# Fourier part of a DiT layer: first group's products copied to SBUF by ScalarE too, differences at another place, reversals and halves moved within the hand-written order

## The chip, the cores and the metric

The kernel runs on one core of one Trainium2 chip. The metric is the device time of one execution in microseconds (us), taken as the median of three runs; the time before is 2893.03 us (2890.24 to 2895.41). A profiled execution gives the rows that are read here: busy times, waits, DMA issues and landings, and the clock that the throttle grants to TensorE.

## What is computed

One layer of a hybrid diffusion backbone, for two streams: 256 prompt tokens and 2048 latent tokens of width 1024. The normalised and modulated input is projected to queries, keys, values and 512 Fourier channels. Four heads of differential attention work on the first three, four groups of 128 channels of a Fourier mixing on the last; both are joined by an output projection, and a squared-ReLU MLP follows. All inputs and outputs are float32. The part that the change touches computes this:

```python
def fourier_mix(f, w_four):
    b, n, _, _ = f.shape
    spec = jnp.fft.fft2(f.astype(jnp.float32), axes=(1, 3), norm='ortho').real.astype(f.dtype)
    return jnp.einsum('bngc,gce->bnge', spec, w_four).reshape(b, n, FOUR_WIDTH)
```

`n` is 256 for the prompt and 2048 for the latent tokens, which are transformed separately.

## The kernel before

The program goes through its stages in order: projection of 18 token tiles of 128 rows (to about 478 us), the Fourier part (to about 537 us), attention (its first product is L1020), then output projection and MLP. Most products of large size are made of three fp32r terms (L88 to L90); the Fourier part uses fp32 matmuls, which run in two passes, so that one 128x512 product shows as two MATMUL rows.

**Folding.** The transform over 2048 positions is a product with cosine and sine matrices. Sums and differences of mirrored and of distant rows split it into smaller ones, named by their size: "2048" (odd part, with the row halves E and DR made at the end of the projection), "e" (1024), "f" (512) and "l" (256). The prompt's 256 rows are the part "p". For the folding, DVE makes the differences `d1024` of the loaded sums `ss` (function diff, L792), the sums (summed, L795), and from a reversal of the rows on PE (reverse, L806 and L808, with the exchange matrices jm and k0) the halves e and o (even_odd, L816, L817, and a copy of one row, L819).

**A part's steps.** For each channel group g of a part, PE makes two position products (pabo at L733 for the 2048-row part, pabe and pabf at L745, pabp and pabl at L753), ScalarE copies them to SBUF (L737, L755), and one step later in the order yT makes two products over channels, py (L698) and pz (L700), whose difference and sum are the rows of the result and of its mirror image. ScalarE copies py to yu (L704). For group 0 of the 2048-row part DVE reads pz from PSUM: yd = yu - pz (L717) and yu = yu + pz (L718); POOL and DVE then write the four quarters of ys0 (L720 to L723). For groups 1 to 3 ScalarE copies pz to yv as well (L707), and the work on yu and yv is put on a list, LATE, and run at a later point of the order; for group 3 it is done by POOL. In the smaller parts DVE reads pz from PSUM at once (L712, L713). The results of the prompt, yp0 to yp3, are stored by POOL's DMA queue as each is ready (L763), those of the latent tokens at the end (L774).

**PSUM.** py, pz, the reversals and the two transposed tiles pt of the last token tile's queries and keys (head_T2, L847) share three buffers of the tag "y". A new tile has to wait until the last reader of the tile that had its buffer is done. The products pabo, pabe and so on have five buffers of their own.

**What sets the order.** From `with tc.manual_schedule()` on, instructions are issued as they are written, so each engine runs its instructions in that order. A table, AFTER, says what is done behind which step: ("o", g) is behind group g of the 2048-row part, ("p", g) behind group g of the prompt part, ("p", 0, 0) ahead of the last results of the part before. SBUF tiles take places that tiles of the projection had; a tile's first write waits for the last reader of what lay there, also where that reader is a store to DRAM. Stores of the last token tiles (queries qd at L355, keys kd at L341, values vd at L370 and vs at L378) stand in SP's queue, and so do the loads of attention (K at L966, V at L972, Q at L994).

Of the kernel before, what the change touches and what calls it, by code (L numbers as in the profile page):

```python
# [11 lines left out]
F32 = mybir.dt.float32  # L12
# [7 lines left out]
P = 128  # L20
D = 1024
KD = D // P
NP = 256
# [18 lines left out]
def body(tc, a, out):  # L42
    nc = tc.nc
    ctx = ExitStack()
    with ctx:
# [184 lines left out]
        with ExitStack() as c1:  # L230
# [358 lines left out]
            with tc.manual_schedule():  # L589
# [12 lines left out]
                def ft32(pool, tag, nm, bufs):  # L602
                    return pool.tile([P, 512], F32, tag=tag, name=nm, bufs=bufs)
# [82 lines left out]
        with ExitStack() as c2:  # L686
            ft = c2.enter_context(tc.tile_pool(name="f_t", bufs=2, reuse_waits="tile"))
            yp = c2.enter_context(tc.tile_pool(name="f_y", bufs=1, reuse_waits="tile"))
            fw = c2.enter_context(tc.tile_pool(name="f_w", bufs=1, side="right", reuse_waits="tile"))
            pp = c2.enter_context(tc.tile_pool(name="f_p", bufs=2, space=PSUM, reuse_waits="tile"))  # L690
            ys = [yp.tile([P, NS], F32, tag=f"ys{g}", name=f"ys{g}") for g in range(4)]
# [2 lines left out]
            def yT(dst, g, A, B, w, mirror_dst, parity=False):  # L694

                r = cw[g]
                py = pp.tile([P, 512], F32, tag="y", name="py", bufs=3)
                nc.tensor.matmul(py[:, :w], r[:, 0, :], A[:, :w], start=True, stop=True)  # L698
                pz = pp.tile([P, 512], F32, tag="y", name="pz", bufs=3)
                nc.tensor.matmul(pz[:, :w], r[:, 1, :], B[:, :w], start=True, stop=True)  # L700

                late = w == 512 and g > 0
                u, v = (fw if late else ft).tile([P, 512], F32, tag="yl" if late else "yu", name="yu", bufs=3 if late else 2)[:, :w], pz[:, :w]
                nc.scalar.copy(u, py[:, :w])  # L704
                if late:
                    v = fw.tile([P, 512], F32, tag="yv", name="yv", bufs=3)
                    nc.scalar.copy(v, pz)  # L707

                def go():
                    if not parity:  # L710
                        c = slice(1, P) if w == HW else slice(0, w)
                        nc.vector.tensor_sub(dst, u, v)  # L712
                        nc.vector.tensor_add(mirror_dst, u[:, c], v[:, c])  # L713
                        return
                    d = ft.tile([P, 512], F32, tag="yd", name="yd", bufs=2)
                    V = nc.gpsimd if g == 3 else nc.vector
                    V.tensor_sub(d, u, v)  # L717
                    V.tensor_add(u, u, v)  # L718
                    de, do, se, so_ = d[:, 0:256], d[:, 256:512], u[:, 0:256], u[:, 256:512]
                    nc.gpsimd.tensor_add(dst[:, 0:256], de, do)  # L720
                    nc.gpsimd.tensor_sub(mirror_dst[:, 511:255:-1], de, do)
                    V.tensor_sub(dst[:, 511:255:-1], se, so_)
                    V.tensor_add(mirror_dst[:, 0:256], se, so_)  # L723

                LATE.append(go) if late else go()
# [32 lines left out]
            HW = P + 1  # L758

            def put_prompt(g, A, B):  # L760
                y = ft.tile([P, NP], F32, tag="yp", name=f"yp{g}", bufs=4)
                yT(y[:, 0:HW], g, A, B, HW, y[:, NP - 1:P:-1])
                nc.gpsimd.dma_start(four[g * P:g * P + P, 0:NP], y)  # L763

# [65 lines left out]
            def late():  # L830
                LATE.pop(0)()

            AFTER = {("o", 0): [(diff, 1024, t) for t in (3, 2, 0, 1)],
                     ("o", 1): [(s_prompt,), (load_mats, "c1024", "s1024", "c512", "s512")],
                     ("o", 3): [(late,), (reverse, 512, 0), (even_odd, 512, 0)],
                     ("p", 0, 0): [(reverse, 512, 1), (even_odd, 512, 1)],
                     ("p", 1): [(summed, 1024, 1), (summed, 1024, 3)], ("p", 2): [(fold, 512, 1)],
                     ("p", 3): [(summed, 1024, 0), (summed, 1024, 2), (fold, 512, 0)],
                     ("e", 0): [(reverse, 256, 0), (late,)], ("e", 1): [(even_odd, 256, 0), (late,)], ("e", 3): [(s_last,)]}

            def after(*at_):
                for fn, *args in AFTER.get(at_, ()):
# [7 lines left out]
            with tc.manual_schedule():  # L850

                ptq = [pp.tile([P, 512], F32, tag="y", name=f"pt{LAST}_{m}", bufs=3) for m in range(2)]
                d1024 = [ft32(ft, "d", f"d1024_{t}", 4) for t in range(4)]
                mats = {nm: [fw.tile([P, a[nm].shape[1]], F32, tag=f"{nm}_{t}", name=f"{nm}_{t}", bufs=1)
                             for t in range(a[nm].shape[0] // P)] for nm in ("c512", "s512", "c1024", "s1024", "c256", "s256")}

                jm, k0 = (fw.tile([P, P], F32, tag=x, name=x) for x in ("jm", "k0"))
                for t in (jm, k0):
                    nc.gpsimd.memset(t, 0.0)
                nc.gpsimd.tensor_copy(jm[:, 1:P], ident[:, P - 1:0:-1])  # L860
                nc.gpsimd.tensor_copy(k0[:, 0:1], ident[:, 0:1])
                pws, paE = [pab("w0")], [pab(f"E{g}") for g in range(4)]
                pws.append(pab("w1"))

                def group_mats(h):
                    for j in range(2):
                        nc.tensor.matmul(pws[h][:, j * 256:j * 256 + P], c128, wf[:, 2 * h + j, :], start=True, stop=True)
                        nc.tensor.matmul(pws[h][:, j * 256 + P:j * 256 + 256], s128, wf[:, 2 * h + j, :], start=True, stop=True)

                def group_parts(h):  # L870
                    r = fw.tile([P, 2, 2, P], F32, tag=f"cw{h}", name=f"cw{h}")
                    nc.scalar.copy(r, pws[h].rearrange("p (g t c) -> p g t c", g=2, t=2))
                    cw.extend(r[:, j] for j in range(2))

                A = [None] * 4

                def e_evac(g):
                    A[g] = evac(paE[g], 0, 512, f"E{g}")

                for t in EROWS:  # L880
                    for g in range(4):
                        ab2048(paE[g], g, t, E[t], com[t], t == EROWS[0], t == EROWS[-1])
                    if t == 2:
                        group_mats(0)
                        group_parts(0)
                group_mats(1)
                e_evac(0)
                group_parts(1)
                e_evac(1)
                load_mats("c256", "s256")  # L890
                pend = None
                for g in range(4):
                    pa = pab(f"o{g}_1")
                    for t in ROWS:
                        ab2048(pa, g, t, DR[t][1], som[t], t == 0, t == 3)
                    B = evac(pa, 1, 512, f"o{g}_1")
                    if g < 2:
                        e_evac(g + 2)
                    if pend:
                        put(2048)(*pend)  # L900
                    pend = g, A[g], B
                    if g in (0, 2):
                        parts[1 - g // 2] = head_T2(g // 2, ptq[g // 2])
                    after("o", g)
                last_put = put(2048)
                for n, (ea, ma, eb, mb), w, p in (
                        ("p", (None, "c256", None, "s256"), HW, put_prompt),
                        ("e", (lambda: EO[512, "e"], "c1024", lambda: EO[512, "o"], "s1024"), 256, put(1024)),
                        ("f", (lambda: EO[256, "e"], "c512", lambda: EO[256, "o"], "s512"), 128, put(512)),
                        ("l", (None, "c256", None, "s256"), HW, put(256))):  # L910
                    for g in range(4):
                        if n in "pl":
                            nA, nB = (ab_half(g, q, (PR, S3)[n == "l"], MT[m][0], n) for q, m in enumerate((ma, mb)))
                        else:
                            nA = ab(g, 0, ea(), MT[ma], w, n)
                            nB = ab(g, 1, eb(), MT[mb], w, n)
                        after(n, g, 0)
                        last_put(*pend)
                        last_put, pend = p, (g, nA, nB)
                        if n == "p" and g == 0:  # L920
                            k_store(0, NK[0] // P - 1, parts[0])
                        if n == "e" and g == 0:
                            q_store(LAST, parts[1])
                        after(n, g)
                last_put(*pend)
# [7 lines left out]
        with ExitStack() as c3_:  # L933
# [265 lines left out]
            u = T / 5.0  # L1199
# [868 lines left out]
```

## Time and profile before

| what | value |
|---|---|
| runs of before | 2890.24, 2893.03, 2895.41 us, median 2893.03 |
| the profiled execution's own time | 2891.59 us |
| its span, first to last instruction | 2889.5 us |
| mean granted TensorE clock | 0.998 |
| busy share of the span | PE 99%, weight loads 85%, DVE 70%, ACT 53%, POOL 37% |
| DMA | 492.93 MB, 170 GB/s over the span |
| first product of attention | 537.08 us |

The span is 2.1 us shorter than the profiled execution's own time, and that time lies 1.4 us under the median of the runs. In the rows, PE is TensorE's matmul stream, DVE is VectorE, ACT is ScalarE, POOL is GpSimd and SP the engine that issues most DMAs; "SPq" and "POOLq" are their DMA issues. A row gives its start, its duration, the engine, the line, the output and the inputs by tile name, and in square brackets how long the engine had been idle and what ended that.

### The profile page before, as it was taken

How to read it: one execution, taken by the hardware profiler on the slowest of the kernel's cores; microseconds unless marked ns; L12 is line 12 of the kernel's file. 1: busy time of each engine (PE TensorE's matmuls, PEld its weight loads, DVE VectorE, ACT ScalarE, POOL GpSimd, SP SyncE). 2: the span in 40 equal slices, each digit the busy share in tenths (PEclk: the TensorE clock that was granted, in tenths of full speed). 3: DMA queues.
4: the chain of work that ended last, by engine and by line, in shares of the span. 5: the costliest groups of instructions: out<-in, count | busy, mean ns of one | idle time of the engine just before them, and what ended most of it. 6: DMA issues, size and time to landing. Idle time of an engine off the chain costs nothing.

```text
span 2889.5 us, 43210 instructions
## 1 busy us (share of the span) xinstructions
PE 2848.0 (99%) x15119; PEld 2468.9 (85%) x15119; DVE 2010.1 (70%) x3375; ACT 1545.7 (53%) x3502; POOL 1060.6 (37%) x869
## 2 busy tenths in 40 slices
PE   8999999999999999999999999999999999999999
PEld 4888787688888888888889999999998888888887
DVE  6676776898998989964478777778775354345554
ACT  4333322699898989953356566556554332233221
POOL 1112113599999999942223333333332000000000
PEclk9999999999999999999999999999999999999999
DMA  7777887521221212136777676667757464445563
GB/s 283 199 200 194 228 212 215 205 103 32 75 80 45 107 43 85 34 112 205 227 227 227 223 250 223 215 225 234 234 170 253 146 200 134 136 142 183 199 208 109
DMA packets 392779, 492.93 MB, mean 171 GB/s; under 512 B 26467, under 2 KB 306384, under 8 KB 389490
## 3 DMA queue, kind: packets, MB, share of 16 engines
q1 hardware_dynamic: 387136, 479.73, 52.6%
q0 software_dynamic: 1872, 7.28, 0.7%
q10 hardware_dynamic: 3554, 3.17, 0.4%
q8 instruction: 119, 1.95, 0.3%
q14 instruction: 98, 0.80, 0.1%
HBM read 312.58 MB, written 179.59 MB: 170 GB/s over the span
## 4 chain that ended last, share of the span: by engine, by line
PE 89%; DVE 4%; DMA 3%; ACT 2%; issue 1%; POOL 1%; SPq 1%; ACTq 0%; DVEq 0%; POOLq 0%
PE Ss L1020 10%; PE ps L89 8%; PE ps L88 8%; PE ps L90 8%; PE pts L1075 5%; PE po L90 4%; PE po L88 4%; PE po L89 4%; PE pj L88 3%; PE pj L89 3%; PE pj L90 3%; PE pA L1683 2%; PE pA L1684 2%; PE pB L1683 2%; PE pB L1684 2%; PE pB L1685 2%
## 5 line engine op out<-in xcount | busy, mean ns | idle before, releaser
L1025 DVE TENSOR_REDUCE mxs<-Ss 128x1 f32<-128x512 f32 x636 | 413.2, 685 | 63.1 <-PE Ss L1020 51.1
L1360 DVE TENSOR_TENSOR sl<-sr,sh 128x768 fp32r<-128x768 f32 x168 | 161.7, 964 | 337.8 <-ACT sh L1359 337.3
L1060 POOL TENSOR_TENSOR P0s<-P0s,P1s 128x1024 f32<-128x1024 f32 (+2 forms) x128 | 378.5, 2957 | 10.7
L1359 ACT CAST sh<-sr 128x768 fp32r<-128x768 f32 x168 | 140.2, 836 | 424.8 <-PE ps L89 423.9
L1725 POOL TENSOR_TENSOR gs<-g,g 128x384 f32<-128x384 f32 x48 | 69.7, 1451 | 469.7 <-ACT g L1695 419.0
L1044 ACT ACTIVATE P1s<-Ss,mxs 128x512 f32<-128x512 f32 x318 | 215.2, 694 | 36.2 <-DVE mxs L1028 36.2
L88 PE MATMUL pj<-wh,hh 128*128 128x512 f32 x576 | 229.4, 398 | 3.9 <-DVE qn L289 3.2
L89 PE MATMUL ps<-tlT,sh 128*128 128x512 f32 x585 | 229.4, 392 | 0.0
L88 PE MATMUL ps<-thT,sh 128*128 128x512 f32 x585 | 229.1, 392 | 0.0
L89 PE MATMUL pj<-wl,hh 128*128 128x512 f32 x576 | 227.7, 395 | 0.6 <-DVE wl L524 0.6
L90 PE MATMUL ps<-thT,sl 128*128 128x512 f32 x585 | 227.8, 389 | 0.0
L90 PE MATMUL pj<-wh,hl 128*128 128x512 f32 x576 | 226.9, 395 | 0.0
L1044 ACT ACTIVATE P0s<-Ss,mxs 128x512 f32<-128x512 f32 x318 | 214.1, 690 | 5.5 <-DVE mxs L1028 4.8
L1020 PE MATMUL Ss<-KS1s,Qs 128*128 128x512 f32 x636 | 196.2, 420 | 6.0 <-ACT P0s L1044 3.4
L1020 PE MATMUL Ss<-KS0s,Qs 128*128 128x512 f32 x636 | 195.5, 420 | 2.6 <-ACT P1s L1044 2.4
L1075 PEld LDWEIGHTS pts<-ident,P0s 128*128 128x128 f32 x1280 | 157.7, 140 | 42.6 <-ACT ahs L1082 2.2
L1075 PE MATMUL pts<-ident,P0s 128*128 128x128 f32 x1280 | 190.4, 272 | 0.7 <-ACT P1s L1044 0.7
L1694 ACT ACTIVATE g<-uz 128x384 f32<-128x384 f32 x144 | 75.8, 527 | 201.1 <-DVE uz L1717 171.4
L1059 POOL TENSOR_SCALAR P1s<-P1s,tots 128x1024 f32<-128x1024 f32 (+2 forms) x128 | 171.7, 1341 | 5.8
L1087 DVE TENSOR_TENSOR als<-pts,ahs 128x512 fp32r<-128x512 f32 x256 | 165.9, 681 | 6.9 <-ACT ahs L1082 6.6
L88 PE MATMUL ps<-ophT,sh 128*128 128x512 f32 x423 | 165.8, 392 | 1.1 <-DVE uz L1717 1.1
L90 PE MATMUL ps<-ophT,sl 128*128 128x512 f32 x423 | 165.8, 392 | 0.0
(533 smaller groups left out, 8057.1 us busy)
## 6 DMA issues: line engine op xcount, KB each, us to landing
sr<-sd SPq DMA_DIRECT2D x84, 768.0 KB
a<-in_w SPq DMA_DIRECT2D x184, 256.0 KB
sd<-gs SPq DMA_DIRECT2D x192, 192.0 KB
sd<-g SPq DMA_DIRECT2D x144, 192.0 KB
wm<-in_w_mod SPq DMA_DIRECT2D x32, 512.0 KB
Qs<-qd SPq DMA_DIRECT2D x32, 512.0 KB
b<-in_w SPq DMA_DIRECT2D x64, 256.0 KB
b<-tsum SPq DMA_DIRECT2D x64, 256.0 KB
```

The source lines that it names most:

```text
L88: nc.tensor.matmul(ps, lh, rh, start=first, stop=False)
L89: nc.tensor.matmul(ps, lh, rl, start=False, stop=False)
L90: nc.tensor.matmul(ps, ll, rh, start=False, stop=last)
L1020: nc.tensor.matmul(S[:, :w], self.Q[:, x, m, j * P:j * P + P], self.hd.KS[m][:, b * 512:b * 512 + w], start=(x == 0), stop=(x == 1))
L1025: nc.vector.tensor_reduce(self.mx[j][:, m, b:b + 1], self.S[j, m, b], axis=AX.X, op=ALU.max)
L1044: nc.scalar.activation(dst, S, AF.Exp, bias=self.mx[j][:, m, 6:7], accum_out=self.sm[j][:, m, b:b + 1])
L1059: nc.gpsimd.tensor_scalar(p, p, tot[:, 3:4], 0.0, op0=ALU.mult, op1=ALU.add)
L1060: nc.gpsimd.tensor_add(d, d, p)
L1075: nc.tensor.transpose(pt[:, c:c + P], self.p0[j][:, (kb + t) * P:(kb + t + 1) * P], ident)
L1087: nc.vector.tensor_sub(t, self.pt[kb], f32(self.A[kb][0]))
L1359: nc.scalar.copy(hi, src)
L1360: nc.vector.tensor_sub(lo, src, f32(hi))
```

## The change

Six edits, all in the Fourier part:

- The tiles yu and yv of the 2048-row part come from a new pool f_l with four buffers each, and `late` holds for group 0 as well: ScalarE copies its pz to yv, and its sums and differences go onto the list LATE, which is run at ("o", 1), behind the prompt's halves.
- The four result tiles of the prompt, YP, are allocated ahead of the differences d1024, in the same pool. By the addresses of the built programs the differences of before lie where vo17 lay, the value tile of the last token tile, which SP stores to vs at L378. Now YP lies there, and the differences lie where qn17 lay. The first Q tile of attention overlaps the place that YP has now.
- In AFTER, the reversal and the halves of 512 part 0 go from ("o", 3) to ("o", 2), those of part 1 from ("p", 0, 0) to ("o", 3), ahead of the LATE entry there; the sums and folds go up by about one step of the prompt part; the 256 reversal goes from ("e", 0) to ("p", 3), its halves from ("e", 1) to ("e", 0).

Behind L688 the lines of the changed kernel are one higher, behind L853 two.

```diff
             yp = c2.enter_context(tc.tile_pool(name="f_y", bufs=1, reuse_waits="tile"))
+            yl = c2.enter_context(tc.tile_pool(name="f_l", bufs=4, reuse_waits="tile"))
...
-                late = w == 512 and g > 0
-                u, v = (fw if late else ft).tile([P, 512], F32, tag="yl" if late else "yu", name="yu", bufs=3 if late else 2)[:, :w], pz[:, :w]
+                late = w == 512
+                u, v = (yl if late else ft).tile([P, 512], F32, tag="yu", name="yu", bufs=4 if late else 2)[:, :w], pz[:, :w]
                 nc.scalar.copy(u, py[:, :w])
                 if late:
-                    v = fw.tile([P, 512], F32, tag="yv", name="yv", bufs=3)
+                    v = yl.tile([P, 512], F32, tag="yv", name="yv", bufs=4)
                     nc.scalar.copy(v, pz)
...
             def put_prompt(g, A, B):
-                y = ft.tile([P, NP], F32, tag="yp", name=f"yp{g}", bufs=4)
+                y = YP[g]
...
-                     ("o", 1): [(s_prompt,), (load_mats, "c1024", "s1024", "c512", "s512")],
-                     ("o", 3): [(late,), (reverse, 512, 0), (even_odd, 512, 0)],
-                     ("p", 0, 0): [(reverse, 512, 1), (even_odd, 512, 1)],
-                     ("p", 1): [(summed, 1024, 1), (summed, 1024, 3)], ("p", 2): [(fold, 512, 1)],
-                     ("p", 3): [(summed, 1024, 0), (summed, 1024, 2), (fold, 512, 0)],
-                     ("e", 0): [(reverse, 256, 0), (late,)], ("e", 1): [(even_odd, 256, 0), (late,)], ("e", 3): [(s_last,)]}
+                     ("o", 1): [(s_prompt,), (late,), (load_mats, "c1024", "s1024", "c512", "s512")],
+                     ("o", 2): [(reverse, 512, 0), (even_odd, 512, 0)],
+                     ("o", 3): [(reverse, 512, 1), (even_odd, 512, 1), (late,)],
+                     ("p", 0): [(summed, 1024, 1), (summed, 1024, 3)], ("p", 1): [(fold, 512, 1)],
+                     ("p", 2): [(summed, 1024, 0), (summed, 1024, 2)], ("p", 3): [(fold, 512, 0), (reverse, 256, 0)],
+                     ("e", 0): [(even_odd, 256, 0), (late,)], ("e", 1): [(late,)], ("e", 3): [(s_last,)]}
...
                 ptq = [pp.tile([P, 512], F32, tag="y", name=f"pt{LAST}_{m}", bufs=3) for m in range(2)]
+                YP = [ft.tile([P, NP], F32, tag="yp", name=f"yp{g}", bufs=4) for g in range(4)]
                 d1024 = [ft32(ft, "d", f"d1024_{t}", 4) for t in range(4)]
```

On PE only three reversals move. This is PE's order before, from the products over channels of group 1 (py, pz) to the second reversal; pt17_1 is a transposition of the last token tile, pabo3 the position products of group 3, rev512 the reversals and fps, fpd the prompt's halves:

```order
L700 MATMUL pz_4784<-abo1_1_4748,cw0_4700 128x512
L847 MATMUL pt17_1_4663<-ident_175,qo17_1_4504 128x128 x4
L733 MATMUL pabo3_1_4798<-s20480_4505,rv0_4514 128x256
...
L698 MATMUL py_4805<-abE2_4729,cw1_4716 128x512
L700 MATMUL pz_4807<-abo2_1_4780,cw1_4716 128x512
L806 MATMUL rev512_0_4820<-d1024_3_4667,jm_4676 128x512
L753 MATMUL pabp0_0_4827<-c256_0_4674,fps_4765 128x65
...
L806 MATMUL rev512_1_4837<-d1024_2_4666,jm_4676 128x512
L808 MATMUL rev512_1_4837<-d1024_3_4667,k0_4677 128x512
```

And PE's order of the change at the same place:

```order
L701 MATMUL pz_4793<-abo1_1_4755,cw0_4707 128x512
L848 MATMUL pt17_1_4666<-ident_175,qo17_1_4504 128x128 x4
L807 MATMUL rev512_0_4807<-d1024_3_4674,jm_4683 128x512
L734 MATMUL pabo3_1_4814<-s20480_4505,rv0_4514 128x256
...
L699 MATMUL py_4821<-abE2_4736,cw1_4723 128x512
L701 MATMUL pz_4823<-abo2_1_4789,cw1_4723 128x512
L807 MATMUL rev512_1_4829<-d1024_2_4673,jm_4683 128x512
L809 MATMUL rev512_1_4829<-d1024_3_4674,k0_4684 128x512
L754 MATMUL pabp0_0_4843<-c256_0_4681,fps_4767 128x65
```

The first reversal now stands ahead of the position products of group 3 instead of behind the channel products of group 2, and the second ahead of the prompt's products instead of behind the first four.

On DVE, this is the order before behind the split of the first transposed tile (qkT17_0l): the four differences, group 0's work with pz in PSUM, the prompt's halves, the split of the second transposed tile, group 1's work:

```order
L792 TENSOR_TENSOR d1024_3_4667<-ss2_4544,ss6_4550 128x512
...
L717 TENSOR_TENSOR yd_4758<-yu_4756,pz_4754 128x512
L718 TENSOR_TENSOR yu_4756<-yu_4756,pz_4754 128x512
...
L782 TENSOR_TENSOR fps_4765<-etmp0_4501,etmp1_4502 128x512
L783 TENSOR_TENSOR fpd_4766<-etmp0_4501,etmp1_4502 128x512
L608 TENSOR_TENSOR qkT17_1l_4795<-pt17_1_4663,qkT17_1h_4794 128x512
L717 TENSOR_TENSOR yd_4813<-yu_4786,yv_4788 128x512
...
L816 TENSOR_TENSOR e512_0_4822<-d1024_0_4664,rev512_0_4820 128x512
...
L816 TENSOR_TENSOR e512_1_4840<-d1024_1_4665,rev512_1_4837 128x512
```

And DVE's order of the change from the same row on:

```order
L793 TENSOR_TENSOR d1024_3_4674<-ss2_4544,ss6_4550 128x512
...
L783 TENSOR_TENSOR fps_4767<-etmp0_4501,etmp1_4502 128x512
L784 TENSOR_TENSOR fpd_4768<-etmp0_4501,etmp1_4502 128x512
L718 TENSOR_TENSOR yd_4771<-yu_4763,yv_4765 128x512
L719 TENSOR_TENSOR yu_4763<-yu_4763,yv_4765 128x512
...
L608 TENSOR_TENSOR qkT17_1l_4804<-pt17_1_4666,qkT17_1h_4803 128x512
L817 TENSOR_TENSOR e512_0_4809<-d1024_0_4671,rev512_0_4807 128x512
...
L817 TENSOR_TENSOR e512_1_4832<-d1024_1_4672,rev512_1_4829 128x512
...
L718 TENSOR_TENSOR yd_4836<-yu_4795,yv_4797 128x512
```

Group 0's sums read yv instead of pz and stand behind the prompt's halves, and the halves of both reversals stand ahead of group 1's work. ACT has one row more, the copy of group 0's pz. On POOL the clearing of jm and k0 stands two rows of work earlier. SP's order is the same.

## The prediction

> **What bounds the kernel now.** I read the page's busy shares first, then the busy time by stretch, then the chain of work that ended last, and last each engine's own rows around the place that the chain points to. In the page:
>
> ```profile
> PE 2848.0 (99%) x15119; PEld 2468.9 (85%) x15119; DVE 2010.1 (70%) x3375; ACT 1545.7 (53%) x3502; POOL 1060.6 (37%) x869
> ```
>
> TensorE (PE) is busy for 99% of the span, so it sets the time as long as it is fed; the change adds no matmul and takes none away, and can only win what PE loses by waiting. Of the stretches below the columns are length, PE busy, weight loads, DVE, ACT, POOL, granted clock, DMA share and GB/s.
>
> ```profile
> 494.96:500.05 5.09, 0.16 (x1) 0.00 (x1) 3.80 (x7) 0.58 (x1) 0.69 (x2) 0.96 0.41 127
> 500.05:503.87 3.82, 3.82 (x13) 3.33 (x14) 3.79 (x7) 0.59 (x1) 3.82 (x8) 0.61 0.36 102
> 510.77:537.08 26.31, 25.09 (x172) 22.74 (x170) 20.57 (x47) 13.36 (x47) 10.86 (x14) 1.00 0.72 254
> 640.00:1200.00 560.00, 555.87 (x3590) 476.77 (x3590) 502.40 (x986) 506.97 (x1425) 511.44 (x415) 1.00 0.19 65
> ```
>
> In the Fourier part there is one hole: from 494.96 to 500.05 PE does nothing (the 0.16 is the tail of the matmul before it), and for the 3.82 us behind it the granted clock is 0.61. From 640 to 1200 PE is busy for 555.87 of 560.00 us: attention is one stream of PE work, so what attention starts earlier should stand at the end of the program too. The chain of work shows what the hole waits for:
>
> ```profile
> 482.92 6.47 DMA etmp<-fp
> ...
> 492.79 0.56 SPq L378
> ...
> 493.94 2.85 DMA vd<-v17l
> 496.79 1.89 DVE d L792 x3
> 499.31 0.70 DVE yu L718
> 500.05 1.11 PE pt L847 x4
> ```
>
> The stores of the last projected tiles leave SP's queue one by one up to 493.94; L378 is `vs<-vo`. Behind them come the differences (L792), then the subtraction and addition of group 0 (L717, L718), and with the end of L718 a transposition on PE. The chain names `vd<-v17l`, which is the store that landed about then; in the allocation the first difference, d1024_3, has the place of vo17, so it must wait for the store `vs<-vo`, issued 1.15 us ahead. That transposition `pt` needs nothing from the differences: it waits since its PSUM buffer was last `pz` of group 0, which DVE reads in L717 and L718, and these stand behind the four differences in DVE's queue. PE's rows:
>
> ```profile
> 487.63 0.60 PE L847 MATMUL pt<-ident,qo 128*128 128x128 f32 x4
> 489.80 1.02 PE L698 MATMUL py<-abE,cw 128*128 128x512 f32 x2
> 494.10 1.02 PE L700 MATMUL pz<-abo,cw 128*128 128x512 f32 x2
> 500.05 1.11 PE L847 MATMUL pt<-ident,qo 128*128 128x128 f32 x4 [4.93 <-DVE yu L718]
> 500.96 2.92 PE L733 MATMUL pabo<-s,rv 128*128 128x256 f32 x8
> 503.71 1.02 PE L698 MATMUL py<-abE,cw 128*128 128x512 f32 x2
> 523.29 0.70 PE L700 MATMUL pz<-abe,cw 128*128 128x256 f32 x2 [0.72 <-DVE ys L713]
> 529.96 0.49 PE L700 MATMUL pz<-abf,cw 128*128 128x128 f32 x2 [0.50 <-DVE ys L713]
> 537.08 2.58 PE L1020 MATMUL Ss<-KS0s,Qs 128*128 128x512 f32 x10
> ```
>
> The hole is dear twice. It costs 500.05 - 494.96 = 5.09 us itself. Then a transposition and eight products, which took 489.80 - 487.63 = 2.17 us at full clock, take 503.71 - 500.05 = 3.66 us: 1.49 us more. Together 6.58 us. The Trainium skill, "TensorE: Matmul & The Clock Gate", section "What's actually happening", has the clock at half after at least one idle window of about 3.4 us and back after about 3.4 busy us; the 4.93 us of idle and the 0.61 here agree. By that rule a rest of the hole under 3.4 us would cost its own length and no clock.
>
> **The change part by part.**
>
> *Copy of group 0's pz by ScalarE.* One more 128x512 copy. ACT's rows:
>
> ```profile
> 490.96 0.60 ACT L704 COPY yu<-py 128x512 f32<-128x512 f32 x1
> 493.50 0.58 ACT L737 COPY abo<-pabo 128x512 f32<-128x512 f32 x1 [1.94 <-PE pabo L733]
> ```
>
> Group 1's two products are copied 0.86 us apart on PE's pace, so group 0's pz can be copied from about 491.8 to 492.4. That falls into the 1.94 us before 493.50, in which ACT waits anyway. It costs nothing, and if the cover were gone it would cost the 0.6 of such a copy. The PSUM buffer is then free at 492.4, and PE gets to `pt` at 494.96: 2.5 us to spare, the wait is gone. Nothing else holds `pt`: its input comes from DVE's rotations, which stand ahead of 489.43 in DVE's queue.
>
> *The place of the differences.* In the allocation d1024 moves to where qn17 lay, whose last readers are those rotations; the prompt's four result tiles YP take vo17's place. The differences then wait only for their loads, and the chain has the last of all these (etmp) landed at 482.92 + 6.47 = 489.39. They can start when DVE is free. DVE's rows:
>
> ```profile
> 489.43 0.69 DVE L608 TENSOR_TENSOR qkT_0l<-pt,qkT_0h 128x512 fp32r<-128x512 f32 x1 [1.78 <-ACT qkT_0h L607]
> 496.18 2.50 DVE L792 TENSOR_TENSOR d<-ss,ss 128x512 f32<-128x512 f32 x4 [6.06 <-DMA vd<-v17h]
> 500.03 0.42 DVE L722 TENSOR_TENSOR ys<-yu 128x256 f32<-128x256 f32 x1
> 503.06 0.68 DVE L717 TENSOR_TENSOR yd<-yu,yv 128x512 f32<-128x512 f32 x1
> 504.50 0.83 DVE L722 TENSOR_TENSOR ys<-yu 128x256 f32<-128x256 f32 x1
> 505.25 0.95 DVE L723 TENSOR_TENSOR ys<-yu 128x256 f32<-128x256 f32 x1
> 509.10 0.69 DVE L816 TENSOR_TENSOR e<-d,rev 128x512 f32<-128x512 f32 x1 [0.87 <-PE rev L808]
> 512.32 0.29 DVE L712 TENSOR_TENSOR yp<-yu,pz 128x129 f32<-128x129 f32 x1 [1.94 <-ACT yu L704]
> 522.17 0.61 DVE L712 TENSOR_TENSOR ys<-yu,pz 128x256 f32<-128x256 f32 x1
> 523.08 0.68 DVE L816 TENSOR_TENSOR e<-d,rev 128x512 f32<-128x512 f32 x1
> 524.38 0.62 DVE L819 COPY o<-d 1x512 f32<-1x512 f32 x1
> 526.69 0.63 DVE L712 TENSOR_TENSOR ys<-yu,pz 128x256 f32<-128x256 f32 x1 [0.67 <-PE pz L700]
> 529.27 0.63 DVE L713 TENSOR_TENSOR ys<-yu,pz 128x256 f32<-128x256 f32 x1
> ```
>
> From 490.12: four differences 2.5, the prompt's two halves 1.2 (half of that), group 0's four operations as group 1's of before (503.06 to 505.25 + 0.95) 3.1, qkT_1l 0.6, and e, o and the one-row copy of the first reversal 1.9 (as 523.08 to 524.38 + 0.62). That gives 499.4.
>
> *Reversals earlier.* PE now runs from 494.96 without the hole and at full clock: pt 0.44, first reversal 0.86, pabo 1.73, py and pz 2 x 0.86, second reversal 2 x 0.86, and it ends at about 501.6 (pairs of 512 columns start 0.86 us apart, and one ends 1.02 behind its start, as at 494.10). The first reversal has its input, d1024_3, at 490.8. DVE, done at 499.4, waits some 2.2 us for the second reversal. This slack also covers an unknown: group 0's sum and difference now read two SBUF tiles, beside POOL's additions. Group 1's rows have that form already, and I take their 3.1 us; anything up to 5.3 would change nothing.
>
> *From 501.6 on DVE is the engine to count*, since work moves onto its front. In before, 509.10 (second e) to 522.17 (first result of the 1024 part) are 13.07 us, of which 1.94 idle: 11.1 of work. Added ahead of that point: group 1's four operations (3.1, which now stand behind the second reversal) and the 256 reversal's e, o and copy (1.9). So 501.6 + 16.1 = 517.7 against 522.17. From there to the end of the last 1024 result before took 529.27 + 0.63 - 522.17 = 7.73, less the 1.9 moved away, less 0.67 idle: 5.2. So 522.9 against 529.90: 7.0 us earlier. There PE waits, as it does now (529.96, 0.50 idle). PE by itself could be there at 529.46 - 6.58 = 522.9, and 0.7 earlier if the wait at 523.29 falls away. Both counts agree within that; the DVE count, 7.0, is the upper figure, and PE's loss in the hole alone, 6.58, the lower, with the other waits as they are. I take **6.8 us**. Behind 529.96 PE works on to 537.08 with no wait, so the first product of attention goes to about 530.3.
>
> *What the moved tiles hold up.* The first Q load of attention lies over the place that YP now has, so on SP it waits until all four prompt results have been stored. The rows are the four stores `four<-yp` (128 KB each) from issue to landing, and two issues of SP's queue:
>
> ```profile
> DMA to landing us min/median/max: 4.7/6.5/6.9
> 501.81 0.58 SPq L341 DMA_DIRECT2D kd<-qkT_1h  x1
> 513.51 0.38 SPq L994 DMA_DIRECT2D Qs<-qd  x1
> ```
>
> The first k store follows pt by 501.81 - 500.05 = 1.76, so SP starts at 496.7 and stands at Qs 11.7 us later, at 508.4. The last prompt result comes at 517.7 - 3.1 - 1.9 = 512.7 (group 2's four operations and the 256 reversal's stand between), its store is issued by 513.3 and lands by 520.2 at 6.9. Q is twice the size of the store that took 2.85 us in the chain; at double that it is there at 525.9, and the first use is at 530.3: 4.4 us to spare. Behind Qs on SP stand V's load, two more Qs and the prompt's K and V, none used at the start of attention. Cost 0. POOL's two memsets and the copies of jm and k0 only change places with waits of POOL's own; ACT's table and DMA issues stay.
>
> **The sum**: 2891.59 - 6.8 = 2884.8 us for the profiled execution; against the median of the runs, 2893.03, it is 2886.2.
>
> **The rivals.** Within 0.2% is 5.8 us, about what a measurement of this kernel can tell from no change, and my gain is only 1 us above it.
>
> 1. *DVE is slower than counted.* From 501.6 to 522.9 DVE has no idle time in my count, and anything added goes straight into the time. Some 40 instructions stand there; 0.05 us more for each is 2.0 us. Gain 4.8, **2888.2**. For it: L722 with the same shapes took 0.42 in group 0 (500.03) and 0.83 in group 1 (504.50), so a duration here can double with what runs beside it. Against it: all rows I used come from this very stretch. 0.18.
> 2. *The place doesn't help, only the copy does* (the change does half of what it says: a load or a store still holds the differences until 496.18). PE then gets to the first reversal at 495.4 and waits for d1024_3 until 496.8, 1.4 us; the stretch with the 0.72 us of idle at 523.29 has the clock at 1.00, so I count no clock lost. DVE ends its four differences at 498.7, and with 1.2 + 3.1 + 0.6 + 1.9 is at the second e at 505.5 rather than 501.6. 6.8 - 3.9 = 2.9: **2890.1**. 0.08, as the chain has the loads down by 489.39.
> 3. *More*: the remaining waits of PE (0.72 + 0.50) go as well, gain 6.8 + 1.2 = 8.0, **2885.0**. It would need DVE faster than its rows: 0.05.
> 4. *Slower*: the Q load stays behind the stores. Attention starts later than now only if the last prompt store lands after 537.08 - 5.7 = 531.4, which is 18 us after its issue, and from there each us costs one; at 24 us after issue it is 2893.03 + 6, **2899**. The rows have 4.7 to 6.9. 0.05. The Trainium skill, "SBUF — State Buffer", section "Who interferes with whom", says that a DMA which seems stalled by DVE is one whose descriptors GpSimd writes, and these stores are of that kind; the four rows beside a busy DVE show no more than 6.9.
> 5. *It does not reach the end*: attention's first loads or exponentials bind and give the start back, about **2892**. Against it are the 555.87 of 560.00 us. 0.04.
>
> **How the numbers follow.** The forecast has 0.60. Faster by over 0.2% (under 2887.2): most of the forecast (0.54), rival 3 (0.05) and the better third of rival 1 (0.06): 0.65. Within: the rest of these, rivals 2 and 5: 0.30. Slower: 0.05. The runs of before lie 5.2 us apart, 2.6 to a side. The low end is rival 3 less that, rounded, 2882; the high end is rival 2 with half of it, 2891, which leaves out the slower case and part of rival 5.
>
> **What would show it.** In the changed profile: no idle of PE over 1 us between 494 and 500, with the clock at 1.00 behind it; ACT's copy of pz near 491.7; the first difference at 490.1, right behind qkT_0l; DVE waiting 2 to 3 us for the second reversal near 501.6; first results of the 1024 part near 517.7; PE's last Fourier wait near 523; SP standing at the first Qs until 519 to 520; the first attention product near 530.3. A Qs that PE waits for, or DVE rows longer than here, would make it wrong.

## The result, and the profile after

The changed kernel takes 2884.68 us in the median of nine runs (2882.42 to 2887.58), where nine runs of the kernel before have 2893.03. The ratio is 0.9972 with a 95% interval of 0.9962 to 0.9982. Its profiled execution took 2886.51 us with a span of 2884.7, so it lies 1.8 us above its median, while that of before lies 1.4 us below its own.

The two executions reach the Fourier part at slightly different times: the first position product of the 2048-row part (`pabo`) starts at 485.91 us before and at 486.87 after. So I measure one **stretch**: from that start to the first product of attention (`Ss`). Before it has 537.08 - 485.91 = 51.17 us. These are PE's rows after:

```profile
486.87 1.89 PE L734 MATMUL pabo<-s,rv 128*128 128x256 f32 x8
...
495.06 1.02 PE L701 MATMUL pz<-abo,cw 128*128 128x512 f32 x2
495.92 0.60 PE L848 MATMUL pt<-ident,qo 128*128 128x128 f32 x4
496.36 1.02 PE L807 MATMUL rev<-d,jm 128*128 128x512 f32 x2
...
524.93 0.49 PE L701 MATMUL pz<-abf,cw 128*128 128x128 f32 x2 [1.49 <-DVE ys L714]
...
532.05 2.58 PE L1022 MATMUL Ss<-KS0s,Qs 128*128 128x512 f32 x10
```

The second transposition `pt` follows pz without idle time, and the stretch is 532.05 - 486.87 = 45.18 us, 5.99 less. From the first attention product to the end of the span it is 2352.4 us before and 2352.6 after: what the Fourier part gains stands at the end. The busy times by stretch (columns as before) show the hole filled and the clock whole:

```profile
495.92:504.99 9.07, 9.07 (x35) 5.51 (x34) 6.39 (x11) 3.95 (x8) 5.08 (x9) 1.00 0.95 267
504.99:532.05 27.06, 25.42 (x171) 23.11 (x170) 23.16 (x50) 13.46 (x47) 13.42 (x16) 1.00 0.77 256
```

On DVE the differences now start where qkT_0l ends, and the last rows show where something was not as counted:

```profile
490.39 0.69 DVE L608 TENSOR_TENSOR qkT_0l<-pt,qkT_0h 128x512 fp32r<-128x512 f32 x1 [2.16 <-ACT qkT_0h L607]
491.00 2.49 DVE L793 TENSOR_TENSOR d<-ss,ss 128x512 f32<-128x512 f32 x4
...
502.58 0.69 DVE L817 TENSOR_TENSOR e<-d,rev 128x512 f32<-128x512 f32 x1 [2.57 <-PE rev L809]
...
518.24 0.62 DVE L713 TENSOR_TENSOR ys<-yu,pz 128x256 f32<-128x256 f32 x1
...
520.67 0.64 DVE L713 TENSOR_TENSOR ys<-yu,pz 128x256 f32<-128x256 f32 x1 [0.39 <-PE pz L701]
...
521.61 1.14 DVE L783 TENSOR_TENSOR s256s<-ss 128x512 f32<-128x512 f32 x1
522.67 1.22 DVE L784 TENSOR_TENSOR s256d<-ss 128x512 f32<-128x512 f32 x1
...
524.26 0.62 DVE L714 TENSOR_TENSOR ys<-yu,pz 128x256 f32<-128x256 f32 x1
```

The halves s256s and s256d of the last part take 1.14 and 1.22 us. PE's 1.49 us at 524.93 is the wait for the result behind them. POOL works at the same time on group 3:

```profile
521.47 0.73 POOL L722 TENSOR_TENSOR ys<-yd 128x256 f32<-128x256 f32 x1
522.15 1.18 POOL L723 TENSOR_TENSOR ys<-yu 128x256 f32<-128x256 f32 x1
523.30 1.18 POOL L724 TENSOR_TENSOR ys<-yu 128x256 f32<-128x256 f32 x1
```

### The profile page after: what moved, and what is told of

Same layout as the page of the kernel before. It is cut to its first block, busy times and chain, and to the rows that moved or that the text cites. A ratio compares the mean times of both kernels' runs of the same rounds, so it can differ in the third digit from the quotient of the medians.

```text
span 2884.7 us, 43207 instructions
## 1 busy us (share of the span) xinstructions
PE 2847.6 (99%) x15119; PEld 2468.6 (86%) x15119; DVE 2011.5 (70%) x3375; ACT 1547.0 (54%) x3503; POOL 1061.7 (37%) x869
## 4 chain that ended last, share of the span: by engine, by line
PE 91%; DVE 3%; ACT 3%; DMA 2%; issue 1%; POOL 0%; SPq 0%; ACTq 0%; DVEq 0%; POOLq 0%
PE Ss L1022 10%; PE ps L88 8%; PE ps L89 8%; PE ps L90 8%; PE pts L1077 5%; PE po L90 4%; PE po L88 4%; PE po L89 4%; PE pj L88 4%; PE pj L89 4%; PE pj L90 4%; PE pA L1685 2%; PE pA L1686 2%; PE pB L1685 2%; PE pB L1686 2%; PE pB L1687 2%
```

## The experiments

The change has three parts: the **place** of the differences, the **copy** of group 0's pz by ScalarE, and the **order** of reversals, halves and sums. The first six runs split them. Theory A is that the place makes all of the gain; theory B that the copy does, as it frees the PSUM buffer for which PE waits; theory C that the order adds its own.

### The place alone

```diff
-                y = ft.tile([P, NP], F32, tag="yp", name=f"yp{g}", bufs=4)
+                y = YP[g]
...
+                YP = [ft.tile([P, NP], F32, tag="yp", name=f"yp{g}", bufs=4) for g in range(4)]
                 d1024 = [ft32(ft, "d", f"d1024_{t}", 4) for t in range(4)]
```

> Only the place of the differences is changed; DVE still reads group 0's pz from PSUM and the order is that of before. Theory A (the store that lies in front of the differences makes the hole, and moving them is enough): the differences start right behind qkT_0l, DVE is through with pz about 1 us before or just as PE gets to the second transposition, so PE idles there for less than 0.3 us, the clock stays at 1.00, and the gain is 6 to 7 us, nearly all of the change. Theory B (the buffer that pz holds makes the hole, and ScalarE's copy is what frees it): pt still waits for DVE for 1.5 us or more, and without the earlier reversals the gain is at most 5 us.

Measured: 2884.92 us against 2893.63 for the kernel before on the same chip, ratio 0.9969 (0.9958 to 0.998). PE's rows, then DVE's:

```profile
485.87 1.89 PE L733 MATMUL pabo<-s,rv 128*128 128x256 f32 x8
...
494.92 0.60 PE L847 MATMUL pt<-ident,qo 128*128 128x128 f32 x4
...
530.38 2.58 PE L1021 MATMUL Ss<-KS0s,Qs 128*128 128x512 f32 x10
```

```profile
490.00 2.49 DVE L792 TENSOR_TENSOR d<-ss,ss 128x512 f32<-128x512 f32 x4
...
493.12 0.69 DVE L718 TENSOR_TENSOR yu<-yu,pz 128x512 f32<-128x512 f32 x1
```

Two lines of the diff give the whole gain: the stretch is 44.51 us, even shorter than with the change. DVE is through with pz at 493.81, and PE gets to pt at 494.92. With the differences on time, 1.1 us are left without any copy. That is theory A, and against B.

### The copy alone

```diff
-                late = w == 512 and g > 0
+                late = w == 512
...
-                     ("o", 1): [(s_prompt,), (load_mats, "c1024", "s1024", "c512", "s512")],
+                     ("o", 1): [(s_prompt,), (late,), (load_mats, "c1024", "s1024", "c512", "s512")],
```

(with the new pool f_l for yu and yv)

> Only ScalarE's copy of group 0's pz, with its sums and differences put off behind the prompt's halves; the differences stay where the store holds them and the reversals stay where they were. Theory A: pt no longer waits, but the hole comes back some 4 us further on, at the first reversal, which waits for a PSUM buffer that DVE frees behind the late differences; PE idles there for about 3.9 us, and the gain is 0.5 to 2.5 us. Theory B: the gain is 5 us or more.

Measured: 2892.87 against 2893.63 us, ratio 0.9996 (0.9987 to 1.0005). PE's row, the stretch behind it, and DVE's first difference:

```profile
504.34 2.08 PE L807 MATMUL rev<-d,jm 128*128 128x512 f32 x2 [5.04 <-DVE qkT_1l L608]
```

```profile
504.34:508.00 3.66, 3.66 (x11) 2.63 (x12) 3.59 (x5) 0.27 (x1) 3.64 (x7) 0.50 0.74 180
```

```profile
496.92 2.50 DVE L793 TENSOR_TENSOR d<-ss,ss 128x512 f32<-128x512 f32 x4 [6.51 <-DMA vs<-vo]
```

The hole has only moved: PE passes pt and then stands for 5.04 us at the first reversal, whose buffer was pt's and waits for DVE's qkT_1l, behind the late differences. The half clock comes with it (0.50). I had expected 3.9 us and a small gain; with 5.04 us the stretch is 52.23 us, no shorter than before, and the medians show no gain that can be told from none. A freed buffer is of no use while the engine that frees the next one is late. DVE's row also names the store that the place stands for, vs<-vo, itself; so do the profiles of the next run, of the order alone and of the second profile of before. The first profile of before had named vd<-v17h, the store issued just behind it.

### Copy and order

The diff of the change without the two lines on YP.

> The copy by ScalarE and the new order of reversals and halves; the differences stay behind the store. Theory A: PE idles in two or three smaller stops instead of one, about 1.1 us at the first reversal for the first difference and 2.8 us at the next pz, none long enough for a slow clock; gain 1.5 to 3 us (rival 2 of the prediction, which had 2.9). Theory B: 5 us or more.

Measured: 2891.65 against 2893.63 us, ratio 0.9994 (0.9985 to 1.0003): no gain that can be told from none. The stretch is 52.35 us, no shorter than before. PE's rows, and the stretches behind the first and behind the second stop:

```profile
496.50 1.10 PE L807 MATMUL rev<-d,jm 128*128 128x512 f32 x2 [2.01 <-DVE d L793]
...
503.07 2.07 PE L701 MATMUL pz<-abo,cw 128*128 128x512 f32 x2 [2.89 <-DVE qkT_1l L608]
```

```profile
496.50:500.02 3.52, 3.52 (x12) 2.17 (x12) 3.49 (x7) 0.58 (x1) 0.00 (x0) 1.00 0.19 37
...
503.07:506.50 3.43, 3.42 (x4) 1.46 (x5) 1.56 (x3) 0.58 (x1) 2.24 (x5) 0.51 0.78 198
```

The stops are where A had them, but the first is larger (2.01 us against 1.1), and the second one, of 2.89 us, does halve the clock: the two matmuls take 2.07 us instead of 1.02. Theory A had counted no clock lost. By the stretch its gain of 1.5 to 3 us is missed; the medians, 2.0 us apart with an interval from 0.9 us longer to 4.3 us shorter, don't decide that. B's 5 us lie outside of it.

### Place and order

The change without the copy.

> The place and the new order; group 0's pz is read from PSUM by DVE as before. Theory A: no idle time at pt, and the time of the change itself within 1 us (gain 6 to 8 us). Theory B: pt waits for DVE, and the gain is 1.5 us or more short of the change's.

Measured: 2885.28 against 2893.63 us, ratio 0.9971 (0.9959 to 0.9983). The first pabo starts at 486.87, as after; these are PE's rows:

```profile
495.92 0.60 PE L847 MATMUL pt<-ident,qo 128*128 128x128 f32 x4
...
524.92 0.49 PE L700 MATMUL pz<-abf,cw 128*128 128x128 f32 x2 [1.49 <-DVE ys L713]
532.04 2.57 PE L1021 MATMUL Ss<-KS0s,Qs 128*128 128x512 f32 x10
```

Row by row it is the changed kernel, with a stretch of 45.17 us: the copy adds nothing that can be seen. And the order with the place is 0.66 us longer than the place alone: the wait of 1.49 us at the end belongs to the order.

### The order alone

The new table AFTER, without `late` at ("o", 1), on the kernel before.

> Only the order of reversals, halves and sums is changed; the differences stay behind the store and DVE reads group 0's pz from PSUM. Theory A (the place alone makes the gain): the hole at the second transposition stays, about 5 us with the slow clock behind it, and the time is that of before within 1.5 us. Theory C (the reorder matters by itself): 2 us or more faster.

Measured: 2894.65 against 2894.21 us, ratio 1.0001 (0.9992 to 1.001). PE's and DVE's rows:

```profile
500.33 1.11 PE L847 MATMUL pt<-ident,qo 128*128 128x128 f32 x4 [4.33 <-DVE yu L718]
...
531.90 0.49 PE L700 MATMUL pz<-abf,cw 128*128 128x128 f32 x2 [1.49 <-DVE ys L713]
```

```profile
528.59 1.12 DVE L782 TENSOR_TENSOR s256s<-ss 128x512 f32<-128x512 f32 x1
529.64 1.22 DVE L783 TENSOR_TENSOR s256d<-ss 128x512 f32<-128x512 f32 x1
```

The hole stays, and the late wait of 1.49 us with the long halves comes with the order alone. Theory C falls.

### Place and copy

The change with the table of before, and `late` at ("o", 1).

> The place and the copy, in the order of before. Theory A: the time of the place alone, about 8 us under before, within 1 us; PE meets no idle time at the second transposition, and its last wait in the Fourier part stays near 0.5 us, since DVE makes the two halves of the 256 part behind POOL's work, not beside it. Theory C: the copy adds to the place, 1.5 us or more.

Measured: 2884.75 against 2894.21 us, ratio 0.9966 (0.9954 to 0.9978); stretch 531.72 - 487.13 = 44.59 us. DVE's halves and PE's last wait:

```profile
522.26 0.69 DVE L783 TENSOR_TENSOR s256s<-ss 128x512 f32<-128x512 f32 x1
522.86 0.69 DVE L784 TENSOR_TENSOR s256d<-ss 128x512 f32<-128x512 f32 x1
```

```profile
524.60 0.49 PE L701 MATMUL pz<-abf,cw 128*128 128x128 f32 x2 [0.52 <-DVE ys L714]
```

As with the place alone. In the old order the halves stand behind POOL's last work and take 0.69 us.

The stretches side by side, each from one profile, with the median against that of before on the same chip:

| parts | stretch, us | median - before, us |
|---|---|---|
| none (before) | 51.17 | |
| order | 52.24 | +0.4 |
| copy | 52.23 | -0.8 |
| copy, order | 52.35 | -2.0 |
| place | 44.51 | -8.7 |
| place, copy | 44.59 | -9.5 |
| place, order | 45.17 | -8.4 |
| all (the change) | 45.18 | -8.4 |

The stretch of before varies from one execution to the next (three profiles, further down, have 50.56 to 51.85 us), so a difference of 1 us among the four kernels without the place says nothing.

### The halves of the 256 part, away from POOL

```diff
-                     ("e", 0): [(even_odd, 256, 0), (late,)], ("e", 1): [(late,)], ("e", 3): [(s_last,)]}
+                     ("e", 0): [(even_odd, 256, 0), (s_last,), (late,)], ("e", 1): [(late,)]}
```

> The changed kernel with the two halves of the 256 part (s256s, s256d) made behind the 256 reversal's halves, where POOL stands idle, rather than beside POOL's work on group 3. Theory D (the two took 1.14 and 1.22 us in the changed kernel because POOL reads SBUF at the time; alone they take 0.68): both take 0.68 to 0.70 us here and PE's wait of 1.49 us at the last result of the 1024 part shrinks below 0.5 us; some of it comes back as a wait of about 1 us at an earlier pz, since DVE's total work is what binds; 0.5 to 1 us gained from the first pabo to attention. Theory E (their length comes from something else, as DMA): they stay over 1 us.

Measured: 2883.44 against 2894.21 us, ratio 0.9963 (0.9951 to 0.9976); stretch 530.46 - 485.90 = 44.56 us, 0.62 less than the change. DVE's, POOL's and PE's rows:

```profile
514.20 0.67 DVE L783 TENSOR_TENSOR s256s<-ss 128x512 f32<-128x512 f32 x1
514.80 0.67 DVE L784 TENSOR_TENSOR s256d<-ss 128x512 f32<-128x512 f32 x1
```

```profile
522.38 0.73 POOL L723 TENSOR_TENSOR ys<-yu 128x256 f32<-128x256 f32 x1
```

```profile
519.61 0.70 PE L701 MATMUL pz<-abe,cw 128*128 128x256 f32 x2 [0.43 <-DVE ys L714]
```

Both sides shrink: DVE's halves to 0.67 us, POOL's subtraction from 1.18 to 0.73. Theory D holds. The late wait is gone, and 0.43 us of it comes back at an earlier pz, where about 1 us had been expected.

### A candidate

```diff
-                     ("o", 2): [(reverse, 512, 0), (even_odd, 512, 0)],
-                     ("o", 3): [(reverse, 512, 1), (even_odd, 512, 1), (late,)],
+                     ("o", 2): [(reverse, 512, 0), (even_odd, 512, 0), (late,)],
+                     ("o", 3): [(reverse, 512, 1), (even_odd, 512, 1)],
...
-                     ("p", 2): [(summed, 1024, 0), (summed, 1024, 2)], ("p", 3): [(fold, 512, 0), (reverse, 256, 0)],
-                     ("e", 0): [(even_odd, 256, 0), (late,)], ("e", 1): [(late,)], ("e", 3): [(s_last,)]}
+                     ("p", 2): [(summed, 1024, 0), (summed, 1024, 2)], ("p", 3): [(fold, 512, 0), (reverse, 256, 0), (s_last,)],
+                     ("e", 0): [(even_odd, 256, 0), (late,)], ("e", 1): [(late,)]}
```

> The changed kernel with DVE's group 1 work put into DVE's idle 2.6 us ahead of the second reversal's halves, and the two halves of the 256 part behind the last fold. By the count of DVE's rows PE's waits of the Fourier part come to about 0.5 us in all instead of 1.9: from the first pabo to attention about 43.2 us instead of 45.2 in the changed kernel and 44.5 with the place alone, so 1.5 to 2 us faster than the change and about 1.2 us faster than the place alone. If something but DVE bound that stretch, it stays at 44.5 to 45.2.

Measured: 2884.06 against 2894.21 us, ratio 0.9962 (0.995 to 0.9975). PE's rows, and the busy times from 503 us to attention:

```profile
485.54 1.89 PE L734 MATMUL pabo<-s,rv 128*128 128x256 f32 x8
...
528.82 2.56 PE L1022 MATMUL Ss<-KS0s,Qs 128*128 128x512 f32 x10
```

```profile
503.00:528.82 25.82, 25.80 (x173) 23.16 (x171) 20.53 (x47) 13.99 (x48) 10.86 (x14) 1.00 0.93 316
```

The stretch is 43.28 us, as counted (43.2), 1.9 less than the change, and PE is busy for 25.80 of the last 25.82 us: there is nothing left to win there but work. The runs can't tell it from the change: it is 10.2 us under its own runs of before and the change 8.4, with intervals (7.2 to 14.5 and 5.2 to 11.0) that overlap. That it is better is shown by its rows only.

### The kernel before, twice more

> The kernel before, unchanged, for a second profile. The runs gained about 8 us, while the two profiles differ by only 6.0 us from the first pabo of the 2048-row part to attention (51.2 and 45.2 us). Theory F: the hole varies from one execution to the next, since it ends on a store that stands behind loads and other stores in a queue, and the first profile had a short one; here the stretch is 52 us or more. Theory G: the hole is the same each time and the rest of the gain is scatter of other stretches; here it is 51.0 to 51.4 us.

> The kernel before once more, for a third profile. Theory F: 51 to 53.5 us from the first pabo to attention, not the same as in the other two, and the time of the first difference moves with it against the first pabo. Theory G: 51.0 to 51.4 us again.

Measured: 2891.52 and 2890.6 us, one execution each. PE's rows of the second profile, then of the third:

```profile
485.03 1.89 PE L733 MATMUL pabo<-s,rv 128*128 128x256 f32 x8
...
498.30 0.66 PE L847 MATMUL pt<-ident,qo 128*128 128x128 f32 x4 [4.05 <-DVE yu L718]
...
535.59 2.58 PE L1020 MATMUL Ss<-KS0s,Qs 128*128 128x512 f32 x10
```

```profile
484.47 1.89 PE L733 MATMUL pabo<-s,rv 128*128 128x256 f32 x8
...
499.04 1.11 PE L847 MATMUL pt<-ident,qo 128*128 128x128 f32 x4 [5.35 <-DVE yu L718]
...
536.32 2.58 PE L1020 MATMUL Ss<-KS0s,Qs 128*128 128x512 f32 x10
```

The stretches are 50.56 and 51.85 us, with 51.17 in the first profile. The hole does vary (4.05, 4.93, 5.35 us of idle), and the stretch with it, around the same 51.2. Theory G, which wanted it fixed, falls. Of theory F the mechanism holds: the first difference starts 9.40, 10.27 and 10.70 us behind the first pabo, in the order of the stretches 50.56, 51.17 and 51.85. But F had also wanted the first profile to be a short one, with 52 us or more in the second, and that fails; so the varying hole doesn't explain why the medians fell by more than the stretch.

## Why the prediction was right, point by point

The forecast was 2886.2 us, the measured median is 2884.68, inside the range and on the side that was forecast. That it comes so near is in part luck: the stretch fell by 0.8 us less than forecast, the median by 1.5 us more.

- *The hole and the slow clock, 6.58 us.* Gone as forecast: no idle time at pt, clock 1.00 behind it.
- *The copy.* It ran where it was put, in idle time of ACT, at no cost. But I let it be what frees the buffer, and that is not so: with the place alone DVE frees it 1.1 us ahead of PE. The part that carries the gain is the place. Rival 2 leaves it 3.9 of the 6.8 us; alone it takes 6.66 us off the stretch, and the copy alone nothing.
- *DVE from 490 to 518.* The first result of the 1024 part was put at 517.7; after has 518.24, which is 517.28 counted from a start 0.96 us earlier as in before. The wait for the second reversal was put at 2.2 us and is 2.57.
- *DVE from there to the last result of the 1024 part, 5.2 us.* This term was mis-sized: it took 524.26 + 0.62 - 518.24 = 6.64 us. Of the 1.4 us more, 0.39 is a wait for PE, and 1.0 is s256s and s256d, which I had taken with the times they have beside an idle POOL. The new order lets DVE catch up with POOL's group 3 work. That is rival 1 in its mechanism, with 1.0 of its 2.0 us, and two DVE rows longer than those of before are what the prediction's last sentence had named as a sign of being wrong. The Trainium skill, "SBUF — State Buffer", section "Who interferes with whom", states that a DVE instruction with two SBUF inputs contends with a GpSimd instruction that reads SBUF; 1.14 and 1.22 us beside POOL against 0.67 and 0.69 alone agree.
- *The stretch*: 6.8 us forecast, 5.99 in the two profiles. The difference is this term's 1.4 us, less the 0.4 by which DVE was earlier than counted ahead of it (517.28 against 517.7), and less the 0.2 by which the forecast stood under DVE's count of 7.0.
- *The Q load behind the prompt's stores.* Forecast to stand until 519 to 520 and to cost nothing. It was issued 13 us ahead of its use:

```profile
519.01 0.32 SPq L996 DMA_DIRECT2D Qs<-qd  x1
```

- *Rival 2, the copy without the place*, was priced at a gain of 2.9 us; the run of copy and order has 2.0 in the medians, with none and 4.3 both in its interval, and a stretch no shorter than before. Two steps failed. It counted one stop of 1.4 us, and there were two, of 2.01 and 2.89 us: the second, at pz, waits for the buffer that qkT_1l frees. And it counted "no clock lost".
- *What stays open.* The medians fell by 8.4 us, the stretch by 6.0; the four kernels with the place fell by 8.4 to 9.5 us, their stretches by 6.0 to 6.7. Each interval takes in its own stretch (the change: 5.2 to 11.0 us), if at its small end each time. Three profiles of before have the same 51.2 us on the mean, and the time behind attention's start is the same in both kernels. The granted clocks of the single runs show that the two profiles are not alike: of the 23 runs of before that went with the first experiments, the six with a mean clock of 0.998 took 2888.77 to 2892.27 us and the 17 with 0.996 or 0.997 took 2892.70 to 2896.00, and all three profiles of before have 0.998. Of the nine runs of the change, the five with 0.999 took 2882.42 to 2884.68 us and the four with 0.998, the profiled one among them, 2885.51 to 2887.58. So shorter executions of before are compared with a longer one of the change, and the two profiled executions differ by 5.1 us, less than the medians. Where in the longer executions of before the clock is lower no profile shows, so I don't name a cause.

## What to carry to other kernels

When an engine stands still for a buffer, ask which instruction would free it and what that one waits for. Here the buffer was held by DVE, DVE by a tile's place, and the place by a store at the end of a long queue; moving the tile ended all three waits, and freeing the buffer alone only moved the hole to the next buffer that DVE frees. And when an order is moved forward, look at what will now run beside it: a duration read beside the old neighbours can come out 1.7 to 1.8 times as long.

## What the runs showed of the hardware

In the run of copy and order, a stop of 2.01 us left TensorE's clock at 1.00; one of 2.89 us, behind 3.7 us of work, brought 0.51 for the next 3.43 us. The prediction quoted the Trainium skill, "TensorE: Matmul & The Clock Gate", section "What's actually happening", with an idle window of about 3.4 us and took a stop below that as free; here, in one run, the measurement differs, and it decides: 2.89 us was long enough. Nor does the length alone say when the clock falls. In the second profile of before it stood at 1.00 through a longer stop, of 4.05 us, and fell only behind it; these are the stretches of the stop and behind it:

```profile
493.90:498.30 4.40, 0.35 (x2) 0.00 (x1) 3.80 (x7) 0.70 (x2) 0.69 (x2) 1.00 0.33 100
498.30:502.00 3.70, 3.70 (x13) 3.12 (x14) 3.68 (x6) 0.62 (x2) 3.70 (x8) 0.64 0.33 91
```

DVE and POOL held each other up here while both read two SBUF inputs: s256s took 1.14 instead of 0.67 us while POOL's subtraction L723 took 1.18 instead of 0.73. The same pair of instructions costs nothing extra when one of them stands elsewhere in the order. The rows look like turns rather than like two engines at a lower pace: POOL's L722, which had started first, keeps its 0.73, and from there the ends alternate, 522.20 (POOL), 522.75 (DVE), 523.33 (POOL), 523.89 (DVE), 524.48 (POOL), each 0.55 to 0.59 us behind the other engine's. The order alone, copy and order, and place and order show the same alternation, with 0.54 to 0.60 us.
